# A hybrid trunk kernel: the recurrence's input and gate projections computed as a group of seven products among the projections of the attention branch

## The chip, the cores and the metric

One Trainium2 chip, one NeuronCore. The kernel is one launch of the whole two-layer trunk. The metric is device time in microseconds (us); the time before is the median of three runs, 1835.72 us (1835.08 to 1836.69). Engines are named as in the profile: PE is the matmul engine, PEld its weight loads, DVE the vector engine, ACT the scalar (activation) engine, POOL the general-purpose engine, which here mostly issues DMAs, and SP the engine that only issues DMAs. Each engine executes its own instructions in program order and waits, at an instruction, for semaphores of the others.

## The reference, cut to what matters

Two layers over 256 tokens of width 2048, in fp32. In each layer one wide projection of the normed rows is split into the inputs of four branches, and every branch result is gated, projected, and summed:

```python
def hybrid_layer(x, ...):
    h = rms_norm(x, norm_g)
    u = h @ w_in                                   # 256 x 2048 times 2048 x 15944
    (a_q, a_k, a_v, a_z, a_qi, a_ki, a_wi, b_q, b_k, b_v, b_z,
     c_f, c_i, c_q, c_z, m_q, m_z, gates) = split_cols(u)
    y_a = sparse_index_attention(...a_q, a_k, a_v, a_qi, a_ki, a_wi)
    y_b = head_rms_norm(retention(rope(b_q), rope(b_k), b_v), ret_g)
    f = lb + (1.0 - lb) * sigmoid(c_f)
    y_c = head_rms_norm(hgrn2(f, c_i, c_q), hgrn_g)          # the recurrence
    y_m = memory_attention(m_q, m_k, m_v)
    for n, (y, z) in enumerate(((y_a, a_z), (y_b, b_z), (y_c, c_z), (y_m, m_z))):
        branch = y * silu(z)
        merged += sigmoid(gates[n]) * (branch @ w_branch[n])
    return x + merged @ w_out
```

The change is about `c_i` (the recurrence's input) and `c_z` (its gate), each 256 x 2048 times 2048 x 512.

## The kernel before

**Slabs and halves.** Weights are streamed from HBM in slabs of 512 rows by 512 columns (1 MB, tile `raw`, four buffers, loaded on SP). Each slab is cut into two halves. For a half, ACT rounds the weights to `whi` (`ac.copy` in `cut_piece`) and DVE subtracts to get the remainder `wlo`; a plain projection then takes, for each of four 128-row blocks of its k and token half, three matmuls of 128x512: hi by hi, hi by lo, lo by hi. That is 12 matmuls a half, output tile `u`. `whi` and `wlo` have four buffers (HL), so the cut of a half can start only when PE has finished the half four places before it. The rows x are kept as `x00h`, `x00l`, and so on (layer, quarter of the 2048, rounded part and remainder).

**Groups of seven products.** For three of the four branches, two of the four column blocks of the gates are computed as one 2 x 2 block product with seven products instead of eight (output tile `px`). The weight combinations, tiles `sum`, are built in place by DMAs: the first block by a plain load on SP, further blocks by accumulating DMAs on POOL, each of which waits for DVE's cut of the tile that it changes (`add_block`). The combinations of x are called s1, s2, r4 and s3 and are made once a layer by `forms`: tile `s`, then a rounded part on ACT (`s1h`, `s2h`, `r4h`, `s3h`) and a remainder on DVE (`s1l`, ...). The s3 form is made in a second, later task. A product is used in two parts of two halves; a half takes 6 matmuls.

**Order.** Python records the program while it runs an account of engine costs. `gemms` and `product` record the matmuls of a half and then call `advance`, which lets the waiting tasks record up to two steps, and then records the cut of the next half. All side work (norms, transposes by DMA called `fold`, selection `ix...`, the recurrence's scores `cq`, `ck`, `cV`, `cin`, retention scores `bs`) is such tasks. `stream.finish(task)` records all that is left of a task at once. What has been recorded is the order on each engine; nothing is rearranged later. The program order of a layer is: the pair CF and CQ, then CI, CZ, QI0 (256 columns wide), QI1 (328), AQ, AK, AV, AZ, MQ, MZ, BQ, BK, BV, BZ, then the gates with their products and the branch projections `bw`, then the output projection `wo`.

**The retention scores.** `bs` is the product of `bqpt` and `bkpt`, two tiles that a `fold` moves in 16 small DMAs each, half on POOL and half on SP. SP's queue also holds the `raw` loads, which wait for the cut that frees their buffer.

Of the kernel before, what the change touches and what calls it, by code (L numbers as in the profile page):

```python
# [235 lines left out]

def mingled(products, side):
    out, total = [], sum(BETWEEN_PRODUCTS) * len(products) // 14
    at = done = 0
    for i in range(len(products) // 2):  # L240
        at += BETWEEN_PRODUCTS[i % 7]
        between = side[done:at * len(side) // total]
        done += len(between)
        inside = between[:len(between) // 2]
        out += [products[2 * i]] + inside + [products[2 * i + 1]] + between[len(inside):]
    return out


def gate_tokens():
    rows, products = [], []  # L250
    for n in BR_ORDER:
        gates = [[("gate", n, d, b) for b in range(4)] for d in range(4)]
        bridges = [("bridge", n, d) for d in range(4)]
        if n in DUO:
            products += [("product", n, i, part) for i in range(7) for part in range(2)]
# [10 lines left out]
def gemm_plan(wmem, win, wbr, wout):  # L266
# [15 lines left out]
    def product(l, n, i, part):  # L282
        stage = CHAINED[i]
        if stage is None:
            slab(win, gate_at(l, n, 2) + (2 + part) * 512 * 512, 512)
            return
        if stage == part == 0:
            starts[len(cuts) - AHEAD] = l, n
        cuts.extend(((l, n), stage, 2 * part + k) for k in range(2))
# [28 lines left out]
def trunk(ctx: ExitStack, tc: tile.TileContext, x, xt, memt, ng, qkg, hg, lbl, win, wmem, wbr, wout,  # L318
# [72 lines left out]
    def split_weights():  # L391
        if stream.cut in starts:
            group = starts[stream.cut]
            chains[group] = [G([128, 2, 512], "sum") for h in range(4)]
            for h in range(4):
                add_block(group, 0, h)
        if cuts[stream.cut]:
            group, stage, h = cuts[stream.cut]
            cut_piece(*half(512), chains[group][h])
            if stage + 1 < len(STAGES):  # L400
                add_block(group, stage + 1, h)
            return
# [4 lines left out]
        cut_piece(hi, lo, raw[:, 2 * j:2 * j + 2, :])  # L407
# [3 lines left out]
    def add_block(group, stage, h):  # L411
        adds, rows, d = STAGES[stage]
        to = chains[group][h].rearrange("p k n -> p (k n)")
        block = dram(win, gate_at(*group, d) + (2 * rows + h // 2) * 512 * 512 + h % 2 * 1024, 2048, 1024)
# [626 lines left out]
    def first_turned(b):  # L1041
# [4 lines left out]
        return split_scaled(raw, ngs[:, 0, 4 * b:4 * b + 4], xtp, "xt", f"x0{b}")  # L1046
# [84 lines left out]
    for l in range(L):  # L1131
# [24 lines left out]
        def loaded_tables(l=l):  # L1156
            yield from stream.rest(60)
            made = [spool.tile([128, 1024], F32, tag="s", name=f"table{i}") for i in range(2)]
# [4 lines left out]
        tables = stream.add(loaded_tables())  # L1163
        br = {}
        early = []
        gates_at = stream.ticks + sum(n for c, n in CHUNKS[:16]) / 64

# [13 lines left out]
        box[key("ci")] = evac(proj(O_CI), rs, "ci")  # L1181
        box[key("cz")] = gate_path(proj(O_CZ), rs, "cz")

        def forms(last=False, key=key):
            made = []

            def held(b, t):
                return [u[:, :, 128 * t:128 * t + 128].bitcast(F32) for u in xh[b]]

            def total(name, first, *signed):  # L1190
                out = first or G([128, 8, 128], name)
                for p in range(2):
                    to = out[:, 4 * p:4 * p + 4, :]
                    terms = [(u, sign) for sign, b, t in signed for u in held(b + p, t)]
                    if first is None:
                        (h, _), (g, sign), *_ = terms[::2]
                        (ve.tensor_add if sign > 0 else ve.tensor_sub)(to, h, g)
                        terms = terms[1::2]
                    for u, sign in terms:
                        yield  # L1200
                        (ve.tensor_add if sign > 0 else ve.tensor_sub)(to, to, u)
# [6 lines left out]
                return out  # L1208

            if last:  # L1210
                yield from wait_for(box, key("bs"))
                yield from total("s3", None, (1, 0, 0), (-1, 0, 1))
                return made
            s1 = yield from total("s1", None, (1, 0, 1), (-1, 2, 1))
            s2 = yield from total("s2", s1, (-1, 0, 0))
            yield from total("r4", s2, (1, 2, 0))
# [6 lines left out]
        stream.add(keep(key("aq"), normed_t(proj(O_AQ), rs, qks[:, l, 0:1], "aq")))  # L1223
        stream.add(keep(key("ak"), normed_t(proj(O_AK), rs, qks[:, l, 1:2], "ak")))
        br[0] = stream.add(attend(box, [key(n) for n in ("aq", "ak", "av", "az", "ix")], "a", gates_at + 40))
        box[key("av")] = evac(proj(O_AV), rs, "av")
        stream.add(keep(key("az"), transposed(gate_path(proj(O_AZ), rs, "az"), "azt")))
# [11 lines left out]
        ready += [stream.add(forms(True))]  # L1239
# [13 lines left out]

        def sigmoid(gt, t, src, rs=rs):
            ac.activation(gt[:, t, :], src, AF.Sigmoid, scale=rs[:, t:t + 1])
# [23 lines left out]
        def plain(b, t):  # L1279
            def form(k):  # L1280
                return [u[:, k % 4, 128 * t:128 * t + 128] for u in xh[b + k // 4]]
            return form

        def summed(i):
            def form(k):
                return [u[:, k, :] for u in ready[i // 3][i % 3]]
            return form

        groups, gates, open_gates = {}, {}, {}

        def open_group():
            stream.claim()
            return PB("px").rearrange("p (t n) -> p t n", t=2), {}, []

        def combined(qs, us, one, ended):
            ve.tensor_tensor(qs, qs, us[:, 0:1, :].to_broadcast([128, 2, 512]), op=OP.subtract)
            yield
            ve.tensor_tensor(us, qs, us[:, 1:2, :].to_broadcast([128, 2, 512]), op=OP.add)
            for t in range(2):
                yield  # L1300
                sigmoid(us, t, us[:, t, :])
            while not ended:
                yield BLOCKED
            ve.tensor_sub(one[:, 1, :], one[:, 1, :], qs[:, 1, :])
            yield
            sigmoid(one, 1, one[:, 1, :])
            return one, us

        FORMS = (lambda: summed(2), lambda: summed(3), lambda: plain(0, 0), lambda: summed(0), lambda: plain(2, 0),
                 lambda: summed(1), lambda: plain(2, 1))  # L1310

        def take(n, i, part):
            if i == part == 0:
                groups[n] = open_group()
            ps, kept_q, ended = groups[n]
            to = ps[:, (0, 1, 0, 1, 0, 1, 0)[i], :]
            product(to, FORMS[i](), part, i != 4, i == 4)
            if not part:
                return
            name = {0: "qs", 2: "us", 4: "gate"}.get(i)  # L1320
            if name:
                kept_q[name] = G([128, 2, 512], name)
            if i in (0, 2, 3, 6):
                name, t = {0: ("qs", 0), 2: ("us", 0), 3: ("us", 1), 6: ("gate", 1)}[i]
                ac.copy(kept_q[name][:, t, :], to)
            elif i == 1:
                ac.activation(kept_q["qs"][:, 1, :], to, AF.Copy, scale=-1.0)
            elif i == 4:
                sigmoid(kept_q["gate"], 0, to)
            else:  # L1330
                us = kept_q["us"]
                ve.tensor_add(us[:, 0, :], to, us[:, 0, :])
                task = stream.add(combined(kept_q["qs"], us, kept_q["gate"], ended))
                gates[n, 2], gates[n, 3] = (task, 0), (task, 1)
            if i == 6:
                ended.append(True)
                del groups[n]
                stream.free()

# [6 lines left out]
        for what, n, *at in gate_tokens():  # L1346
            if what == "product":
                for j, task in enumerate(ready):
                    if isinstance(task, Task) and (j == 0 or at[0]):
                        ready[j] = stream.finish(task)  # L1350
# [6 lines left out]
        def turned(c, xc, nssq, l=l):  # L1357
            u = yield from transposed(xc, "xp")
            r = split_scaled(u, ngs[:, l + 1, 4 * c:4 * c + 4], xtp, "xt", f"x1{c}")
            for t in range(2):  # L1360
# [81 lines left out]
```

## Time and profile before

| | |
|---|---|
| median of 3 runs | 1835.72 us (1835.08 to 1836.69) |
| the profiled execution's own time | 1837.45 us |
| its span, first to last instruction | 1835.7 us |
| mean granted PE clock | 0.999 |
| PE busy | 1825.5 us, 99% |
| DVE busy | 1286.2 us, 70% |
| ACT busy | 972.8 us, 53% |
| POOL busy | 337.1 us, 18% |
| moved by DMA | 428.38 MB, mean 233 GB/s |

The profiled execution took 1.73 us more than the median of the runs. PE is busy all through, so the time is nearly the sum of its matmuls, and the other engines matter only where PE waits for them. A busy duration of a matmul contains its pipeline, so the step from one matmul's start to the next is shorter than its duration; for the chain of work, pieces of many matmuls give the step.

### The profile page before, as it was taken

Reading aid. Unit: us, or ns where it says so; the run is one execution under the profiler, and the core shown is the slowest. Engines: PE = TensorE matmul, PEld = TensorE weight load, DVE = VectorE, ACT = ScalarE, POOL = GpSimd, SP = SyncE. Lnnn points to the kernel's source line nnn. Section 1 sums busy time; section 2 is a strip of 40 time slices with the busy share of each in tenths; the row PEclk is TensorE's granted clock in tenths of the full one; section 3 lists DMA queues with packets and bytes.
Section 4 is the critical chain, followed back from the end, with each engine's and each line's share of the span. In section 5 each row is a group of like instructions: output and inputs, shape, how many; then the busy total and the mean of one; then the engine's idle time right before and its main releaser. Section 6 shows DMA issues by size and latency. Waiting matters only on the chain.

```text
span 1835.7 us, 24214 instructions
## 1 busy us (share of the span) xinstructions
PE 1825.5 (99%) x8932; PEld 1518.1 (83%) x8932; DVE 1286.2 (70%) x1406; ACT 972.8 (53%) x1139; POOL 337.1 (18%) x501
## 2 busy tenths in 40 slices
PE   9999999999999999999999999999999999999999
PEld 8888888888888888888888888888888888888887
DVE  5655878777666767687665587887766676768764
ACT  5654555545365656554445454554545565555542
POOL 0022024214021011103131201421402111110310
PEclk9999999999999999999999999999999999999999
DMA  8776668778699898987797566886869989898873
GB/s 333 271 235 171 235 212 212 217 209 210 199 252 274 251 254 264 262 232 222 234 267 236 167 232 210 212 237 210 216 203 275 259 250 260 257 259 239 219 238 140
DMA packets 186568, 428.38 MB, mean 233 GB/s; under 512 B 114256, under 2 KB 115536, under 8 KB 150608
## 3 DMA queue, kind: packets, MB, share of 16 engines
q1 hardware_dynamic: 160048, 364.27, 61.3%
q0 software_dynamic: 26112, 62.29, 18.3%
q8 instruction: 70, 1.15, 0.3%
q14 instruction: 50, 0.41, 0.1%
q10 hardware_dynamic: 288, 0.26, 0.0%
HBM read 397.64 MB, written 5.24 MB: 219 GB/s over the span
## 4 chain that ended last, share of the span: by engine, by line
PE 93%; DMA 3%; DVE 1%; ACT 1%; issue 1%; SPq 0%; POOL 0%; DVEq 0%; ACTq 0%
PE u L145 57%; PE px L145 11%; PE bw L145 10%; PE wo L145 8%; PE mv L145 2%; PE mk L145 2%; DMA raw<-in_win 1%; DMA xp<-xpi 1%; DVE wlo L127 1%; ACT whi L127 1%; DMA bkpt<-bkpti 0%; DMA apT<-apT1i 0%; PE bs L145 0%; PE ixrp L145 0%; PE mlg L145 0%
## 5 line engine op out<-in xcount | busy, mean ns | idle before, releaser
L127 DVE TENSOR_TENSOR wlo<-raw,whi 128x1024 fp32r<-128x1024 f32 (+3 forms) x604 | 714.7, 1189 | 421.2 <-ACT whi L127 413.1
L127 ACT CAST whi<-raw 128x1024 fp32r<-128x1024 f32 (+3 forms) x604 | 620.1, 1029 | 684.7 <-PE u L145 460.8
L127 DVE TENSOR_TENSOR wlo<-sum,whi 128x1024 fp32r<-128x1024 f32 x144 | 174.0, 1223 | 63.6 <-ACT whi L127 58.6
L127 ACT CAST whi<-sum 128x1024 fp32r<-128x1024 f32 x144 | 151.3, 1055 | 86.4 <-PE u L145 39.4
L127 POOL DMA_DIRECT2D sum<-in_win x96 | 83.5, 870 | 520.1 <-DVE wlo L127 514.4
L145 PE MATMUL u<-whi,x03h 128*128 128x512 f32 (+2 forms) x208 | 80.0, 385 | 0.0
L145 PE MATMUL u<-whi,x13h 128*128 128x512 f32 (+2 forms) x208 | 80.0, 385 | 0.0
L145 PE MATMUL u<-wlo,x00h 128*128 128x512 f32 (+2 forms) x208 | 79.6, 383 | 0.2 <-DVE wlo L127 0.2
L145 PE MATMUL u<-whi,x10h 128*128 128x512 f32 (+2 forms) x208 | 79.8, 384 | 0.0
L145 PE MATMUL u<-wlo,x10h 128*128 128x512 f32 (+2 forms) x208 | 79.6, 383 | 0.2 <-DVE wlo L127 0.2
L145 PE MATMUL u<-whi,x00h 128*128 128x512 f32 (+2 forms) x208 | 79.8, 384 | 0.0
L145 PE MATMUL u<-whi,x02h 128*128 128x512 f32 (+2 forms) x208 | 79.8, 384 | 0.0
L145 PE MATMUL u<-whi,x12h 128*128 128x512 f32 (+2 forms) x208 | 79.8, 384 | 0.0
L145 PE MATMUL u<-whi,x01h 128*128 128x512 f32 (+2 forms) x208 | 79.7, 383 | 0.0
L145 PE MATMUL u<-whi,x11h 128*128 128x512 f32 (+2 forms) x208 | 79.7, 383 | 0.0
L145 PE MATMUL u<-wlo,x13h 128*128 128x512 f32 (+2 forms) x208 | 79.5, 382 | 0.0
L145 PE MATMUL u<-whi,x13l 128*128 128x512 f32 (+2 forms) x208 | 79.5, 382 | 0.0
L145 PE MATMUL u<-wlo,x01h 128*128 128x512 f32 (+2 forms) x208 | 79.5, 382 | 0.0
L145 PE MATMUL u<-wlo,x11h 128*128 128x512 f32 (+2 forms) x208 | 79.5, 382 | 0.0
L145 PE MATMUL u<-whi,x00l 128*128 128x512 f32 (+2 forms) x208 | 79.5, 382 | 0.0
L145 PE MATMUL u<-wlo,x12h 128*128 128x512 f32 (+2 forms) x208 | 79.5, 382 | 0.0
L145 PE MATMUL u<-wlo,x02h 128*128 128x512 f32 (+2 forms) x208 | 79.5, 382 | 0.0
(507 smaller groups left out, 4265.8 us busy)
## 6 DMA issues: line engine op xcount, KB each, us to landing
raw<-in_win SPq DMA_DIRECT2D x204, 1024.0 KB, 5.6
sum<-in_win POOLq DMA_DIRECT2D x96, 512.0 KB, 7.7
raw<-in_wbr SPq DMA_DIRECT2D x32, 1024.0 KB, 6.6
raw<-in_wout SPq DMA_DIRECT2D x32, 1024.0 KB, 5.9
sum<-in_win SPq DMA_DIRECT2D x48, 512.0 KB, 7.0
raw<-in_wmem SPq DMA_DIRECT2D x12, 1024.0 KB, 5.1
raw<-in_win SPq DMA_DIRECT2D x8, 656.0 KB, 4.4
xc<-in_x SPq DMA_DIRECT2D x8, 512.0 KB, 6.8
```

What stands on the lines that cost most here:

```text
L127: return call(*args, **kw)
L145: return self.engine.matmul(out, w, x, **kw)
```

## The change

For each layer, CI and CZ are no longer plain projections. They become a group "c" of seven products, with the same forms of x that the gate groups use. The group's products are put among QI0, QI1, AQ, AK, AV and AZ after the first four slabs (all of QI0, `EARLY`). CI and CZ are left out of the order between CQ and QI0.

- `forms` is one task, with s3 included. It reads x in fp32: the tile of x (`xr`, in the second layer `xp`) is scaled in place on ACT by a task `scaling` and kept, so a form takes one DVE operation per half tile, where it took one for the rounded parts and one more for each remainder. `take` finishes the task before the layer's first product.
- The product that runs on a plain slab moves from place 4 to place 5 of a group (`RING`). In group "c" the last block of the weight sum is added by DVE from that slab, and not by a DMA.
- The two tables of the retention scores sit in general buffers and are loaded at a set tick.
- `retain` rests one more tick; the numbers of side rows between products (`BETWEEN_PRODUCTS`) differ.

In all PE has 48 matmuls of 128x512 fewer (384 of `u` go, 336 of `px` come). DVE has 24 cuts of slabs fewer and 48 cuts of sums more, 24 form operations fewer and 8 additions to sums more; ACT has 24 and 48 such cuts, and 32 scalings of 128x256 more. POOL has 24 accumulating DMAs more, SP 12 slab loads fewer and 16 loads of a sum's first block more.

```diff
-STAGES = ((False, 1, 3), (True, 0, 3), (False, 0, 2), (True, 0, 3), (True, 1, 3), (True, 1, 2))
-CHAINED = (0, 1, 2, 3, None, 4, 5)
-BETWEEN_PRODUCTS = (4, 3, 4, 3, 2, 4, 3)
+STAGES = ((False, 1, 1), (True, 0, 1), (False, 0, 0), (True, 0, 1), (True, 1, 1))
+LAST_SUM, RING, EARLY = (True, 1, 0), 5, 4
+BETWEEN_PRODUCTS = (4, 3, 4, 4, 3, 2, 3)
...
+def columns(l, group):
+    if group == "c":
+        return [l * DM * INW + CHUNK_AT[c] for c in (O_CI, O_CZ)]
+    return [gate_at(l, group, d) for d in (2, 3)]
...
+def early_tokens():
+    rows = [("chunk", c, n, b) for c, n in CHUNKS[4:10] for b in range(4)]
+    return rows[:EARLY] + mingled(products_of("c"), rows[EARLY:])
...
         pair(PAIR_ORDER, *((win, l * DM * INW + CHUNK_AT[c]) for c in (O_CF, O_CQ)))
-        for c, n in CHUNKS[2:16]:
+        for what, *at in early_tokens():
+            if what == "product":
+                product(l, *at)
+            else:
+                c, n, b = at
+                slab(win, l * DM * INW + CHUNK_AT[c] + b * 512 * n, n)
+        for c, n in CHUNKS[10:16]:
             add(win, l * DM * INW + CHUNK_AT[c], n)
...
+        piece = raw[:, 2 * j:2 * j + 2, :]
+        cut_piece(hi, lo, piece)
+        if group and group[1] == "c":
+            ve.tensor_add(chains[group][h], chains[group][h], piece)
...
-        return split_scaled(raw, ngs[:, 0, 4 * b:4 * b + 4], xtp, "xt", f"x0{b}")
+        r = split_scaled(raw, ngs[:, 0, 4 * b:4 * b + 4], xtp, "xt", f"x0{b}")
+        stream.add(scaling(raw, 0, b))
+        return r
+
+    def scaling(u, l, b):
+        for k in range(4):
+            if k % 2 == 0:
+                yield
+            ac.activation(u[:, k, :], u[:, k, :], AF.Copy, scale=ngs[:, l, 4 * b + k:4 * b + k + 1])
+        rows_of[l, b] = u
...
         def retain():
             q = yield from wait_for(box, key("bq"))
             k = yield from wait_for(box, key("bk"))
+            yield from stream.rest(1)
...
-        box[key("ci")] = evac(proj(O_CI), rs, "ci")
-        box[key("cz")] = gate_path(proj(O_CZ), rs, "cz")
...
+            def total(name, out, sign, first, second):
+                for p in range(2):
...
+                    yield
+                    (ve.tensor_add if sign > 0 else ve.tensor_sub)(at, a, b)
+
+            def parts(name, out):
+                hi, lo = (spool.tile([128, 8, 128], F32R, tag="s", name=name + e) for e in "hl")
+                yield
+                ac.copy(hi, out)
+                yield
+                ve.tensor_sub(lo, out, hi.bitcast(F32))
+                made.append((hi, lo))
...
+            one = G([128, 8, 128], "s1")
+            yield from total("s1", one, -1, a21, a22)
+            yield from parts("s1", one)
+            yield from total("s2", one, -1, one, a11)
+            yield from parts("s2", one)
+            yield from total("r4", one, 1, one, a12)
+            yield from parts("r4", one)
+            yield from total("s3", one, -1, a11, a21)
+            yield from parts("s3", one)
...
         ready = [stream.add(forms())]
...
+        def take(group, i, part):
+            if isinstance(ready[0], Task):
+                ready[:] = stream.finish(ready[0])
...
+            form = (summed(2), summed(3), plain(0, 0), summed(0), summed(1), plain(2, 0), plain(2, 1))[i]
+            product(to, form, part, i != RING, i == RING)
...
+        def early_slabs(c0, n=512, l=l):
+            tiles = None
+            for b in range(4):
+                while tokens[0][0] == "product":
+                    take(*tokens.popleft()[1:])
...
+                tiles = gemms(xh, [(win, l * DM * INW + CHUNK_AT[c0])], n, ["u"], order=[(0, b, j) for j in range(2)], tiles=tiles)
+            return tiles[0]
...
-        qi0 = evac(proj(O_QI, 256), rs, "qi0", 256)
-        qi1 = evac(proj(O_QI + 256, 328), rs, "qi1", 328)
+        qi0 = evac(early_slabs(O_QI, 256), rs, "qi0", 256)
+        qi1 = evac(early_slabs(O_QI + 256, 328), rs, "qi1", 328)
...
-        ready += [stream.add(forms(True))]
```

The next rows are the order of instructions, first on DVE from the end of QI0's cuts (128x512) into QI1's (128x656) in the first layer, as the program was; `s_1526` is the tile in which the forms are built, `cq`, `cown` and `ck` belong to the recurrence.

```order
61 L127 TENSOR_TENSOR wlo<-raw,whi 128x512 x4
62 L127 SCALAR_TENSOR_TENSOR czzs<-u,rs0r,czsg 128x512 x2
63 L127 TENSOR_TENSOR s_1526<-x00h,x02h 128x512
64 L127 TENSOR_TENSOR wlo<-raw,whi 128x512 x2
65 L127 TENSOR_TENSOR s_1526<-s_1526,x00l 128x512
66 L127 TENSOR_TENSOR wlo<-raw,whi 128x512 x2
67 L127 TENSOR_TENSOR s_1526<-s_1526,x02l 128x512
68 L127 TENSOR_TENSOR wlo<-raw,whi 128x656
69 L127 TENSOR_TENSOR s_1526<-x01h,x03h 128x512
70 L127 TENSOR_TENSOR wlo<-raw,whi 128x656
71 L127 TENSOR_TENSOR cq<-cq_1432,cf 128x1024
72 L127 TENSOR_TENSOR s_1526<-s_1526,x01l 128x512
```

A form's operations stood singly between the cuts. The same place of the changed program; here `s_1219` is the tile of the forms, and the last row's cuts are of the third and fourth block of the group's first sum.

```order
60 L127 TENSOR_TENSOR wlo<-raw,whi 128x512
61 L127 TENSOR_TENSOR wlo<-sum,whi 128x1024 x2
62 L127 TENSOR_TENSOR s1l<-s_1219,s1h 128x1024
63 L127 TENSOR_TENSOR wlo<-raw,whi 128x656 x2
64 L127 TENSOR_TENSOR s_1219<-s_1219,xr 128x512 x2
65 L127 TENSOR_TENSOR s2l<-s_1219,s2h 128x1024
66 L127 TENSOR_TENSOR s_1219<-s_1219,xr 128x512 x2
67 L127 TENSOR_TENSOR r4l<-s_1219,r4h 128x1024
68 L127 TENSOR_TENSOR s_1219<-xr 128x512 x2
69 L127 TENSOR_TENSOR s3l<-s_1219,s3h 128x1024
70 L127 TENSOR_TENSOR wlo<-sum,whi 128x1024 x2
```

All of s2, r4 and s3 now stands in one piece behind two cuts of QI1's first slab. On PE of the changed program the first product follows the last matmul of QI0, and its first matmuls read `r4h` and, in the third, `r4l`:

```order
677 L145 MATMUL u<-whi,x03h 128x256
678 L145 MATMUL u<-wlo,x03h 128x256
679 L145 MATMUL u<-whi,x03l 128x256
680 L145 MATMUL px<-whi,r4h 128x512
681 L145 MATMUL px<-wlo,r4h 128x512
682 L145 MATMUL px<-whi,r4l 128x512
```

Where QI0 was followed by QI1, the first product now stands between them. SP's queue in the first layer, before BZ ends, with the moves of `bkpt` (for the retention scores) and the slab loads, as it was:

```order
114 L521 DMA mpT_3905<-mpT1i 32x8x32
115 L521 DMA bkpt<-bkpti 32x8x32 x2
116 L374 DMA raw<-in_win 128x2048
117 L521 DMA bkpt<-bkpti 32x8x32 x5
118 L374 DMA raw<-in_win 128x2048
119 L521 DMA bkpt<-bkpti 32x8x32
```

and as it is:

```order
112 L545 DMA apT_3847<-apT1i 32x8x32 x5
113 L393 DMA raw<-in_wbr 128x2048
114 L545 DMA bkpt<-bkpti 32x8x32 x5
115 L393 DMA raw<-in_win 128x2048
116 L545 DMA bkpt<-bkpti 32x8x32 x3
```

The last slab load ahead of the last move of `bkpt` waits for a cut. Before, the half of that cut is used by PE 11 matmuls of 128x512 ahead of `bs`; now 47 such matmuls ahead (with 8 small ones of the attention), and in the second layer 59 where it was 11. Last, DVE in the first layer just before the fifth product's result is taken up (`us<-px`), where the additions to the sums stand:

```order
136 L127 TENSOR_TENSOR wlo<-raw,whi 128x1024 x2
137 L127 TENSOR_TENSOR cq<-cq,cT_2136 128x256x2
138 L127 TENSOR_TENSOR ck<-ck,cT_2136 128x256x2
139 L127 TENSOR_TENSOR cT_2317<-cT_2136 128x256
140 L127 TENSOR_TENSOR wlo<-raw,whi 128x1024
141 L127 TENSOR_TENSOR sum<-sum,raw 128x1024
142 L127 TENSOR_TENSOR wlo<-raw,whi 128x1024
143 L127 TENSOR_TENSOR sum<-sum,raw 128x1024
144 L127 TENSOR_TENSOR us<-px,us 128x512
```

The rows `sum<-sum,raw` and this place of `us<-px` are new; the recurrence's operations of the kernel before stood among cuts of plain slabs and the forms.

More of the change, by code (lines that the diff above doesn't have):

```diff
@@ L254, in gate_tokens @@
         if n in DUO:
-            products += [("product", n, i, part) for i in range(7) for part in range(2)]
+            products += products_of(n)
         if n == BR_ORDER[-1]:
@@ L280, in pair, with product @@
             slab(src, off + b * 512 * 512, 512)
[L282 to L289, printed above, removed]
+    def product(l, group, i, part):
+        if i == RING:
+            p.append((win, columns(l, group)[0] + (2 + part) * 512 * 512, 512))
+        elif i == part == 0:
+            starts[len(cuts) - AHEAD] = l, group
+        cuts.extend(((l, group), i, 2 * part + k) for k in range(2))
     for b in range(4):
@@ L1153, in retain, with loaded_tables @@
             k = yield from wait_for(box, key("bk"))
+            yield from stream.rest(1)
             return (yield from retention_scores(q, k, "b", tables.value))
-        def loaded_tables(l=l):
-            yield from stream.rest(60)
-            made = [spool.tile([128, 1024], F32, tag="s", name=f"table{i}") for i in range(2)]
+        def loaded_tables(until):
+            while stream.ticks < until:
+                yield BLOCKED
+            made = [G([128, 1024], f"table{i}") for i in range(2)]
             for i, to in enumerate(made):
@@ L1180, in trunk, with forms @@
         br[2] = stream.add(mixed("cs", "ci", "cz", 1, "c", gates_at + 3))
-        box[key("ci")] = evac(proj(O_CI), rs, "ci")
-        box[key("cz")] = gate_path(proj(O_CZ), rs, "cz")
-        def forms(last=False, key=key):
+        def forms(l=l):
+            rows = []
+            for b in range(4):
+                rows.append((yield from wait_for(rows_of, (l, b))))
             made = []
[L1187 to L1191, printed above, removed]
+            def total(name, out, sign, first, second):
                 for p in range(2):
[L1193 to L1201, printed above, removed]
+                    at, a, b = (u[p] if isinstance(u, tuple) else u[:, 4 * p:4 * p + 4, :] for u in (out, first, second))
                     yield
+                    (ve.tensor_add if sign > 0 else ve.tensor_sub)(at, a, b)
+            def parts(name, out):
                 hi, lo = (spool.tile([128, 8, 128], F32R, tag="s", name=name + e) for e in "hl")
+                yield
                 ac.copy(hi, out)
@@ L1207, in total @@
                 made.append((hi, lo))
[L1208 to L1216, printed above, removed]
+            a11, a12, a21, a22 = (tuple(rows[b + p][:, :, 128 * t:128 * t + 128] for p in range(2))
+                                  for t in range(2) for b in (0, 2))
@@ L1221, in trunk, with sigmoid, scale_rows, plain @@
[L1221 removed]
+        def sigmoid(gt, t, src):
+            ac.activation(gt[:, t, :], src, AF.Sigmoid, scale=rs[:, t:t + 1])
+        def scale_rows(u, t, src):
+            ac.activation(u[:, t, :], src, AF.Copy, scale=rs[:, t:t + 1])
+        def plain(b, t):
+            def form(k):
+                return [u[:, k % 4, 128 * t:128 * t + 128] for u in xh[b + k // 4]]
+            return form
+        def summed(i):
+            def form(k):
+                return [u[:, k, :] for u in ready[i]]
+            return form
@@ new lines, in trunk, with open_group, combined @@
+        groups, gates, open_gates = {}, {}, {}
+        def open_group():
+            stream.claim()
+            return PB("px").rearrange("p (t n) -> p t n", t=2), {}, []
+        def combined(parts, ended, first, second):
+            qs, us = parts["qs"], parts["us"]
+            ve.tensor_tensor(qs, qs, us[:, 0:1, :].to_broadcast([128, 2, 512]), op=OP.subtract)
+            yield
+            ve.tensor_tensor(us, qs, us[:, 1:2, :].to_broadcast([128, 2, 512]), op=OP.add)
+            yield
+            second = yield from second(us)
+            while not ended:
+                yield BLOCKED
+            one = parts["one"]
+            ve.tensor_sub(one[:, 1, :], one[:, 1, :], qs[:, 1, :])
+            yield
+            first(one, 1, one[:, 1, :])
+            return one, second
@@ new lines, in both, with gated_path @@
+        def both(us):
+            for t in range(2):
+                sigmoid(us, t, us[:, t, :])
+                yield
+            return us
+        def gated_path(us):
+            yield
+            return gate_path(us, rs, "cz")
+        def take(group, i, part):
+            if isinstance(ready[0], Task):
+                ready[:] = stream.finish(ready[0])
+            if i == part == 0:
+                groups[group] = open_group()
+            ps, parts, ended = groups[group]
+            first, second = (scale_rows, gated_path) if group == "c" else (sigmoid, both)
+            to = ps[:, (0, 1, 0, 1, 1, 0, 1)[i], :]
+            form = (summed(2), summed(3), plain(0, 0), summed(0), summed(1), plain(2, 0), plain(2, 1))[i]
+            product(to, form, part, i != RING, i == RING)
+            if not part:
+                return
+            name = {0: "qs", 2: "us", RING: "one"}.get(i)
+            if name:
+                parts[name] = G([128, 2, 512], name)
+            if i in (0, 2, 3, 6):
+                name, t = {0: ("qs", 0), 2: ("us", 0), 3: ("us", 1), 6: ("one", 1)}[i]
+                ac.copy(parts[name][:, t, :], to)
+            elif i == 1:
+                ac.activation(parts["qs"][:, 1, :], to, AF.Copy, scale=-1.0)
+            elif i == RING:
+                first(parts["one"], 0, to)
+            else:
+                us = parts["us"]
+                ve.tensor_add(us[:, 0, :], to, us[:, 0, :])
+                task = stream.add(combined(parts, ended, first, second))
+                gates[group, 2], gates[group, 3] = (task, 0), (task, 1)
+            if i == 6:
+                ended.append(True)
+                del groups[group]
+                stream.free()
@@ new lines, in trunk, with from_group @@
+        tokens = deque(early_tokens())
+        def early_slabs(c0, n=512, l=l):
+            tiles = None
+            for b in range(4):
+                while tokens[0][0] == "product":
+                    take(*tokens.popleft()[1:])
+                assert tokens.popleft() == ("chunk", c0, n, b)
+                tiles = gemms(xh, [(win, l * DM * INW + CHUNK_AT[c0])], n, ["u"], order=[(0, b, j) for j in range(2)], tiles=tiles)
+            return tiles[0]
+        def from_group():
+            task, _ = gates[("c", 2)]
+            while not task.done:
+                yield BLOCKED
+            box[key("ci")], box[key("cz")] = task.value
@@ L1295, in combined @@
[L1295 to L1338, printed above, removed]
```

51 lines of the change are left out of this document (21 added, 30 removed).

## The prediction

> **What bounds the kernel now.** I read the page's busy times first, then PE's waits, then the chain that ended last, and only then single stretches of the timeline.
>
> ```profile
> PE 1825.5 (99%) x8932; PEld 1518.1 (83%) x8932; DVE 1286.2 (70%) x1406; ACT 972.8 (53%) x1139; POOL 337.1 (18%) x501
> PE bs L145 <- DMA apT<-apT1i: 3.4, 2, 2.5
> PE heat L145 <- DVE warm L127: 1.1, 1, 1.1
> PE wo L145 <- DVE wlo L127: 0.5, 1, 0.5
> ```
>
> The second to fourth lines are waits: total, times, longest. PE is busy 99% of the span, and the only wait of PE worth naming is that of `bs`. So two things can move the time: the number of matmuls, and any stall that PE does not have now. In the chain that ended last, a product of one part and a plain slab read:
>
> ```profile
> 510.12 2.75 PE px L145 x12
> 512.87 5.44 PE u L145 x24
> ```
>
> (start, us, what). 24 matmuls of 128x512 in 5.44 us are 226.7 ns each, and 12 of a product take 2.75, so a product's matmul costs what a plain one does.
>
> **Fewer matmuls.** 384 of `u` go and 336 of `px` come: 48 x 0.2267 = 10.9 us less on PE, which is the path. This term is the surest of all.
>
> **The wait of `bs`.** In the timeline of PE (and SP's queue) around it, first layer and then second:
>
> ```profile
> 457.06 0.93 SPq L521 DMA_DIRECT2D bkpt<-bkpti  x1
> 462.81 0.39 PE L145 MATMUL u<-whi,x03l 128*128 128x512 f32 x1
> 465.65 3.46 PE L145 MATMUL bs<-bqpt,bkpt 128*128 128x256 f32 x8 [2.45 <-DMA apT<-apT1i]
> 468.77 0.58 PE L145 MATMUL bw<-whi,cnh 128*128 128x512 f32 x1
> 1334.26 0.39 PE L145 MATMUL u<-whi,x13l 128*128 128x512 f32 x1
> 1335.56 1.97 PE L145 MATMUL bs<-bqpt,bkpt 128*128 128x256 f32 x8 [0.91 <-DMA apT<-apT1i]
> 1337.17 0.59 PE L145 MATMUL bw<-whi,cnh 128*128 128x512 f32 x1
> ```
>
> A matmul that starts at 462.81 makes way 0.23 later, at 463.04, so PE stood idle 2.61 us; in the second layer, from 1334.49, 1.07. There is a second price. The same eight records took 3.12 us until `bw` began in the first layer and 1.61 in the second: 1.51 more, half speed after an idle of 2.61 and none after 1.07. Together 5.2 us. The releaser that the row names is in the same queues as `bkpt`, which `bs` reads; its last move was issued at 457.06. In the new order the slab load ahead of that move waits for a cut that lies 36 matmuls farther ahead of `bs` in the first layer (47 against 11) and 48 in the second: 8.2 and 10.9 us more lead against 2.61 and 1.07 of wait. I take the wait as gone, -5.2. Ends: -5.2, and 0 if some other move is late there instead.
>
> **The forms, in front of the first product.** This is the term that decides. In the new order on DVE, s2, r4 and s3 stand in one piece behind the two cuts of 128x656. The second of those cuts needs the buffer of QI0's last half, so ACT can start it only when PE has finished that half; call this moment T. But PE's next matmul after T is the first product, which reads `r4h`, and its third reads `r4l`. PE must wait from T until s2, its two parts, r4 and its two parts are made one after another. In the kernel before, the forms' operations stood singly between cuts and were needed only some 320 us later by the gates. The rows:
>
> ```profile
> L127 ACT CAST whi<-raw 128x656 fp32r<-128x656 f32 x16 | 11.9, 744 | 10.9 <-PE u L145 10.7
> L127 ACT CAST r4h<-s 128x1024 fp32r<-128x1024 f32 x2 | 2.1, 1042 | 0.0
> L127 DVE TENSOR_TENSOR wlo<-raw,whi 128x656 fp32r<-128x656 f32 x16 | 13.0, 834 | 1.0 <-ACT whi L127 1.0
> L127 DVE TENSOR_TENSOR s<-s,x01l 128x512 f32<-128x512 f32 x4 | 2.7, 684 | 0.0
> L127 DVE TENSOR_TENSOR s1l<-s,s1h 128x1024 fp32r<-128x1024 f32 x2 | 2.4, 1218 | 0.0
> L127 DVE TENSOR_TENSOR r4l<-s,r4h 128x1024 fp32r<-128x1024 f32 x2 | 2.4, 1218 | 0.0
> ...
> 179.78 0.28 PE L145 MATMUL u<-whi,x00l 128*128 128x256 f32 x1
> 180.50 0.28 PE L145 MATMUL u<-whi,x00l 128*128 128x256 f32 x1
> ...
> 189.16 0.84 DVE L127 TENSOR_TENSOR wlo<-raw,whi 128x656 fp32r<-128x656 f32 x1
> 189.92 1.22 DVE L127 TENSOR_TENSOR cq<-cq,cf 128x1024 f32<-128x1024 f32 x1
> ...
> 209.01 1.22 DVE L127 TENSOR_TENSOR wlo<-raw,whi 128x1024 fp32r<-128x1024 f32 x1
> 210.14 0.68 DVE L127 TENSOR_TENSOR s<-s,x00l 128x512 f32<-128x512 f32 x1
> 210.74 1.22 DVE L127 TENSOR_TENSOR wlo<-raw,whi 128x1024 fp32r<-128x1024 f32 x1
> ```
>
> The first six are groups (busy, mean ns of one). The others are starts: operations of DVE that do not depend on each other follow at 1.13 (from 209.01 to 210.14) for 1.22, 0.60 for 0.68, 0.76 for 0.84; a dependent one waits the full duration. A half of QI0 is 12 matmuls of 0.12 (six steps from 179.78 to 180.50), 1.4 us, about the 1.22 of a cut of a sum: so DVE comes to T with the two cuts of sums just done and `s1l` running, by my count with 0.85 of it left. From there: 0.85 + 2 x 0.76 for the cuts, s2 0.60 + 0.68, `s2h` 1.04 on ACT, `s2l` 1.22, r4 0.60 + 0.68, `r4h` 1.04, `r4l` 1.22: 9.45, and five changes of engine or dependent starts of some 0.03 make 9.6. Without the forms the third matmul would have come 0.45 after T, so PE loses 9.1 in each layer, 18.2 in both. Lower end, with `s1l` and the first of the cuts done at T: 0.74 + 0.83 + 7.08 - 0.45 = 8.2. Upper end, with all of `s1l` behind T and no overlap: 9.85. s3 follows on DVE, but behind the first part PE has two ready halves of QI1, and s3's 3.5 us and the next cut fit in; nothing is added.
>
> **The clock behind that stall.** `bs` lost 1.51 after 2.61 us of idle, so after 9 us I add 1.5 for each layer, 3.0. Ends: 0, and 1.7 each, since the program's start ran at half speed for about 3.4 us:
>
> ```profile
> 1.12 3.35 PE L145 MATMUL heat<-warm 128*128 128x128 f32 x14 [1.12 <-DVE warm L127]
> ```
>
> The Trainium skill, page "TensorE: Matmul & The Clock Gate", Part 1, has a clock that falls to half after at least one idle window of about 3.4 us and is granted in full after one busy window of the same length. The `bs` row differs for the fall, since 2.61 us of idle had sufficed. By the page's rule the removal of `bs`'s wait would be worth 3.7 and not 5.2, and the sum below would come out 1.5 higher; I go by the row.
>
> **DVE between the fourth and the fifth product.** DVE gets more here: cuts of sums, additions to sums, and at the same time selection and recurrence. The longest run without slack that I find in the new order goes from behind a cut of a sum to `us<-px`, for which PE's sixth product waits: 14 cuts, 2 additions, 16 steps of selection, 21 others.
>
> ```profile
> L127 DVE TENSOR_TENSOR wlo<-raw,whi 128x1024 fp32r<-128x1024 f32 x565 | 686.7, 1220 | 404.4 <-ACT whi L127 396.4 <-DMA apT<-apT0i 3.0 <-DMA mgp<-mgpi 1.5
> L127 DVE TENSOR_TENSOR acc<-acc,gate 128x1024 f32<-128x1024 f32 x18 | 22.0, 1225 | 0.6
> L127 DVE SCALAR_TENSOR_TENSOR ixsc<-ixrl,ixw,ixsc 128x128 f32<-128x128 f32 x14 | 4.9, 352 | 0.5
> L127 DVE MAX8 ixm<-ixsc 128x8 f32<-128x128 f32 x16 | 4.6, 285 | 0.0
> ...
> L145 PE MATMUL ixrp<-ixkt,ixqt 64*32 64x128 f32 x128 | 2.3, 274 | 0.0
> L145 PE MATMUL cl<-cV,ck 128*32 128x48 f32 x256 | 3.5, 208 | 0.0
> L145 PE MATMUL cdg<-cown,ones 128*32 128x256 f32 x16 | 1.3, 391 | 0.0
> ...
> 184.00:194.00 10.00, 10.00 (x81) 10.00 (x80) 9.79 (x14) 5.71 (x9) 0.00 (x0) 1.00 0.81 263
> ```
>
> 16 x 1.22 = 19.6; selection 8 x 0.35 + 8 x 0.28 = 5.1; the others, 3 of a full tile at 1.22, 7 of half a tile at 0.68 and 11 of an estimated 0.35, 12.3: 37 us, behind 2.3 for the first cut's release. PE has 156 matmuls (35.4) and half of `ixrp`'s 2.3, a quarter of `cl`'s 3.5 and about 1.1 of `cdg`: 38.5. So DVE would be 0.8 late by durations, and on time by starts, which come some 0.08 earlier for about half of them. The last row (a window; third number after the bar of times: DVE) shows DVE 9.79 of 10 us busy with PE at 10.00. I take 0; ends 0 and 2 for both layers.
>
> **What else moves.** ACT's 24 more cuts, 32 scalings and table loads lie beside PE: ACT is 53% busy and PE never waits for it. POOL's 24 more accumulating DMAs and SP's 16 loads wait in the queues in which the `fold` moves stand too:
>
> ```profile
> sum<-in_win POOLq DMA_DIRECT2D x96, 512.0 KB, 7.7
> POOL sum L127 <- DVE wlo L127: 514.4, 79, 22.3
> ```
>
> A sum's block lands 7.7 us after its issue, and POOL stands waiting at such an issue for DVE's cut; moves behind it go later. Sums that are added to now have at least 15 us of PE's work until their next cut, by my count of the order, so they land in time. A late move costs what `bs` shows, 2.6 and 1.5. I take 0; ends 0 (a gain is excluded, since no wait of this kind is left to remove) and 8, two late moves.
>
> **The sum.** -10.9 - 5.2 + 18.2 + 3.0 = +5.1. The sum stands on the profiled execution, whose span is 1835.7 and whose own time is 1837.45, 1.73 above the median of the runs; the difference is added to the median: 1835.7 + 5.1 = 1840.8 us.
>
> **The rivals.**
> - *Faster: the forms are hidden.* If r4 is made while QI0 still runs, only -10.9 - 5.2 are left: 1819.6. For it: in the trace a form's steps are recorded early and singly. Against it: the rows of the new order, in which the steps stand behind a cut that waits for T. It decides once the stall is below 6.2 us a layer, of which r4's part alone (0.60 + 0.68 + 1.04 + 1.22) is 3.5; s2's three steps would have to lie ahead of T. 0.12.
> - *No change.* The stall at its lower end, 16.4, with the clock's loss absent or small: -16.1 + 16.4 + (0 to 3.0) = +0.3 to +3.3, 1836 to 1839. For it: the ends of the two terms; against it: 1.51 after an idle a quarter as long. 0.23.
> - *Slower by far: late transfers take over the place of `bs`.* In the early group the recurrence's and the selection's moves share POOL with adds that wait. Two or three waits as long as that of `bs`, 4.1 each with its clock: 1840.8 + 8 to 12 = 1849 to 1853. For it: POOL's 514 us of waiting at these issues; against it: none of the gates' 96 such adds made PE wait. 0.15.
>
> **How the numbers follow.** My forecast, slower with the stall of the forms as its mark, has 0.50; its own range is 1839.4 to 1846. A change below 0.2%, 3.7 us, is about what a measurement of this kernel cannot tell from none. Slower: 0.50 + 0.15 = 0.65; within 0.2%: 0.23; faster: 0.12. The range leaves out most of the hidden case below and the worst of late transfers above: 1831 to 1851.
>
> **What would show it.** In the changed profile: a wait of PE at `px` for `r4h` or `r4l` (ACT or DVE), two times, 8 to 10 us each, near 150 us and near 1010; half clock in PE's row behind each; no wait at `bs`; no wait at `px` for `us<-px` above 1 us; the chain in time with pieces of DVE `r4l` and `s2l`. I am wrong if PE runs through from `u` 128x256 to `px`, if `bs` still waits, or if waits for DMAs at the recurrence or the selection appear.

## The result, and the profile after

The changed kernel took 1858.58 us (median of four runs, 1857.49 to 1860.1) against 1836.2 us; ratio 1.012, 95% interval 1.0102 to 1.0137. It is slower by 22.4 us, 1.2%. The forecast was slower, 1840.8, range 1831 to 1851: the sign is right, the size missed by 17.8 us. The profiled executions differ by 20.5 us in their spans (1835.7 and 1856.2). Of the thirteen runs of the kernel before that were timed beside run 10 below, two were in a slower state (2018.53 and 3740.36 us) and are left out of its comparison.

The page's busy times and PE's waits of the changed kernel (total, times, longest):

```profile
PE 1822.1 (98%) x8884; PEld 1512.2 (81%) x8884; DVE 1316.0 (71%) x1422; ACT 1019.4 (55%) x1209; POOL 361.0 (19%) x525
PE px L145 <- ACT r4h L127: 16.7, 2, 8.6
PE u L145 <- DVE wlo L127: 6.2, 3, 5.5
PE wo L145 <- DVE gate L127: 1.7, 1, 1.7
PE px L145 <- DVE us L127: 1.6, 1, 1.6
PE alg L145 <- ACT akpt L127: 1.0, 1, 1.0
```

PE has 48 records fewer, and `bs` no longer appears among the waits. Two new ones are large: the wait for `r4h`, once a layer, and one of DVE's cuts. The first in the timeline of DVE, ACT and PE:

```profile
147.95 1.22 DVE L127 TENSOR_TENSOR s1l<-s,s1h 128x1024 fp32r<-128x1024 f32 x1
149.09 1.59 DVE L127 TENSOR_TENSOR wlo<-raw,whi 128x656 fp32r<-128x656 f32 x2
150.59 1.29 DVE L127 TENSOR_TENSOR s<-s,xr 128x512 f32<-128x512 f32 x2
152.99 1.23 DVE L127 TENSOR_TENSOR s2l<-s,s2h 128x1024 fp32r<-128x1024 f32 x1 [1.11 <-ACT s2h L127]
156.66 1.23 DVE L127 TENSOR_TENSOR r4l<-s,r4h 128x1024 fp32r<-128x1024 f32 x1 [1.11 <-ACT r4h L127]
148.55 0.74 ACT L127 CAST whi<-raw 128x656 fp32r<-128x656 f32 x1 [0.65 <-PE u L145]
155.58 1.04 ACT L127 CAST r4h<-s 128x1024 fp32r<-128x1024 f32 x1 [2.62 <-DVE s L127]
148.23 0.28 PE L145 MATMUL u<-whi,x03l 128*128 128x256 f32 x1
156.68 0.79 PE L145 MATMUL px<-whi,r4h 128*128 128x512 f32 x1 [8.17 <-ACT r4h L127]
157.94 0.79 PE L145 MATMUL px<-whi,r4l 128*128 128x512 f32 x1
160.66 0.63 PE L145 MATMUL px<-whi,r4l 128*128 128x512 f32 x1
161.09 0.63 PE L145 MATMUL px<-whi,r4h 128*128 128x512 f32 x1
```

QI0 makes way on PE at 148.35; `r4l` starts 8.31 later, and the third matmul 9.59 later, as the chain had been added up (9.97 later in the second layer). Matmuls then follow at 0.43 instead of 0.227 until 161.9: half speed for 5.3 us. The second wait lies in the second layer, in DVE's rows and then PE's:

```profile
1091.15 1.23 DVE L127 TENSOR_TENSOR wlo<-raw,whi 128x1024 fp32r<-128x1024 f32 x1 [1.96 <-ACT whi L127]
1099.69 1.23 DVE L127 TENSOR_TENSOR cq<-cq,cf 128x1024 f32<-128x1024 f32 x1 [7.32 <-DMA ixqt<-ixqti]
1100.84 1.21 DVE L127 TENSOR_REDUCE aqss<-aqsq 128x8 f32<-128x1024 f32 x1
1102.16 3.49 DVE L127 TENSOR_TENSOR wlo<-raw,whi 128x1024 fp32r<-128x1024 f32 x3
1097.58 0.39 PE L145 MATMUL u<-whi,x11h 128*128 128x512 f32 x1
1103.44 0.79 PE L145 MATMUL u<-wlo,x11h 128*128 128x512 f32 x1 [5.46 <-DVE wlo L127]
```

DVE stands 7.32 us at the recurrence's multiplication, whose input `cq` has been moved by DMA (the releaser named is a move of another tile that landed within 0.1 us of the last one of `cq`); the cuts queue behind it, and PE stops. In the first layer the same multiplication waits 5.00, without PE stopping. How long the 32 moves of that tile take from issue to landing, before and after, and one row of a table by stretch for each (in order: PE, PEld, DVE, ACT, POOL, then PE's clock, DMA share, GB/s):

```profile
DMA to landing us min/median/max: 1.9/3.1/4.5
DMA to landing us min/median/max: 5.3/7.9/15.4
...
1065.00:1100.00 35.00, 35.00 (x254) 30.46 (x253) 30.29 (x45) 18.77 (x24) 4.24 (x8) 1.00 0.68 237
1065.00:1100.00 35.00, 32.97 (x146) 26.95 (x144) 18.87 (x21) 19.43 (x20) 18.73 (x29) 1.00 1.02 233
```

The DMA engines are busy all the time there (1.02 against 0.68) and move no more than before (233 GB/s against 237). The kernel before moves its `cq` of that layer earlier, in the stretch from 1036 to 1052 us, where the share was 0.54. That load is what the prediction lacked.

**The ledger.** Matmuls -10.9, `bs` -5.2. The forms: 148.23 to 162.18 is 13.95 us for steps that take 2.84, so 11.1 lost; in the second layer, 1023.12 to 1036.80, 10.8. The late `cq`: 5.6 of idle and 2.0 at half speed, 7.6. `us` 1.7, `gate` at `wo` 1.9 (a wait of 0.7 at another place of `wo` is gone), `alg` 1.1. Sum +17.4 of the 20.5 of the spans; the other 3.1 us were not traced. The expectations of the experiments below were written with 11.4 and 11.1 for the forms and 8.3 for `cq`, somewhat more than this count.

### The profile page after: what moved, and what is told of

Its sections match the earlier page's. It is cut to its first block, busy times and chain, and to the rows that moved or that the text cites. A ratio compares the mean times of both kernels' runs of the same rounds, so it can differ in the third digit from the quotient of the medians.

```text
span 1856.2 us, 24285 instructions
## 1 busy us (share of the span) xinstructions
PE 1822.1 (98%) x8884; PEld 1512.2 (81%) x8884; DVE 1316.0 (71%) x1422; ACT 1019.4 (55%) x1209; POOL 361.0 (19%) x525
## 4 chain that ended last, share of the span: by engine, by line
PE 89%; DVE 5%; DMA 3%; ACT 1%; issue 1%; SPq 0%; ACTq 0%; DVEq 0%
PE u L145 49%; PE px L145 14%; PE wo L145 9%; PE bw L145 9%; DVE wlo L127 2%; PE mv L145 2%; PE mk L145 2%; DMA cq<-cq0i 1%; ACT whi L127 1%; DMA raw<-in_win 0%; DVE ixsc L127 0%; DMA ixqt<-ixqti 0%; SPq L545 0%; PE mlg L145 0%; PE mov L145 0%
## 5 line engine op out<-in xcount | busy, mean ns | idle before, releaser
L127 DVE TENSOR_TENSOR wlo<-raw,whi 128x1024 fp32r<-128x1024 f32 (+3 forms) x580 | 685.8, 1189 | 401.2 <-ACT whi L127 393.4
L127 ACT CAST whi<-raw 128x1024 fp32r<-128x1024 f32 (+3 forms) x580 | 593.2, 1026 | 631.2 <-PE u L145 406.5
L127 DVE TENSOR_TENSOR wlo<-sum,whi 128x1024 fp32r<-128x1024 f32 x192 | 232.1, 1223 | 66.6 <-ACT whi L127 59.3
L127 ACT CAST whi<-sum 128x1024 fp32r<-128x1024 f32 x192 | 201.2, 1053 | 115.0 <-PE u L145 62.1
L127 POOL DMA_DIRECT2D sum<-in_win x120 | 108.3, 903 | 637.8 <-DVE wlo L127 631.8
L145 PE MATMUL u<-whi,x11l 128*128 128x512 f32 (+2 forms) x192 | 74.0, 385 | 0.0
L145 PE MATMUL u<-whi,x03h 128*128 128x512 f32 (+2 forms) x192 | 73.6, 383 | 0.0
L145 PE MATMUL u<-whi,x00h 128*128 128x512 f32 (+2 forms) x192 | 73.5, 383 | 0.0
L145 PE MATMUL u<-whi,x10h 128*128 128x512 f32 (+2 forms) x192 | 73.4, 383 | 0.0
L145 PE MATMUL u<-whi,x02h 128*128 128x512 f32 (+2 forms) x192 | 73.4, 382 | 0.0
```

What stands on the lines that cost most here:

```text
L127: return call(*args, **kw)
L145: return self.engine.matmul(out, w, x, **kw)
```

## The experiments

Runs 7 and 10 were timed four and ten times, the others once. Four runs of the changed kernel differ by 2.6 us and the four of run 7 by 6.4, so smaller differences between single runs show nothing.

**1 to 4: the two waits, each alone and together.** First, the forms' task is started before CF and CQ:

```diff
+        ready = [stream.add(forms())]
         early.append(rs)
         gemms(xh, [... for c in (O_CF, O_CQ)], ...)
...
-        ready = [stream.add(forms())]
```

> The forms' task is started before CF and CQ, so that s2 and r4 stand between earlier cuts; all else is the changed kernel. Theory one (the two waits for r4 cost 11.4 and 11.1 us, idle and half clock together): both waits vanish, 1858.6 - 22.5 = about 1836. Rival (the forms' work is only moved and DVE holds PE elsewhere): less than half of that, over 1847.

It took 1860.48, no gain at all. In the second layer nothing moved (the steps came no earlier in its order: x itself is finished only at the layer's start), and the 8.6 us stayed. In the first layer the wait for `r4h` was gone, and another, in which PE stood idle for 6.1 us, came 18 us later (DVE, then PE; the last row is DVE in the changed kernel):

```profile
160.86 1.23 DVE L127 TENSOR_TENSOR wlo<-sum,whi 128x1024 fp32r<-128x1024 f32 x1 [1.25 <-ACT whi L127]
171.50 1.38 DVE L127 TENSOR_SCALAR cf<-cf,olb,lbv 128x256 f32<-128x256 f32 x4 [9.41 <-DMA raw<-in_win]
172.80 1.22 DVE L127 TENSOR_TENSOR wlo<-sum,whi 128x1024 fp32r<-128x1024 f32 x1
166.13 0.40 PE L145 MATMUL px<-whi,s3l 128*128 128x512 f32 x1
172.46 0.80 PE L145 MATMUL px<-whi,s3h 128*128 128x512 f32 x1 [5.92 <-ACT whi L127]
...
191.26 1.38 DVE L127 TENSOR_SCALAR cf<-cf,olb,lbv 128x256 f32<-128x256 f32 x4 [1.15 <-ACT cf L127]
```

The recurrence's other moved tile, `cf`, lands late too: up to 15.4 us after its issue, 11.8 in the changed kernel and 7.2 in the kernel before. But the edit also moved the operation that waits. DVE takes `cf` up behind 7 cuts after `s3l` in run 1 and behind 17 in the changed kernel, at 171.5 us and at 191.3: with the forms recorded early, the recurrence's steps are recorded earlier too (in the second layer, where the forms did not move, it stays at 17). So this wait came with the edit, and nothing here shows that the forms' stall had hidden it. What the forms' two waits are worth alone stays open; a run that takes them away and leaves `cf` in its place was not made.

Second, the recurrence takes up its moved q later:

```diff
         q0 = yield from transposed(uq, name + "q0")
+        yield from stream.rest(4)
```

> Changed kernel, but the recurrence takes up its moved q tile four ticks later, so that DVE does not stand waiting for the moves. Theory one (the stall of 8.3 us near 1098 us in the second layer is DVE held up at one operation by transfers that land late): it vanishes, about 1850, the forms' waits unchanged. Rival (DVE has too much work there): the stall stays within 2 us of its size, about 1858.

1851.36, 7.2 less, and the wait at the cut is gone (PE waits for DVE's cuts of `u` 0.4 in all); the forms' 16.7 is unchanged. DVE's amount of work is the same, so it was one operation that waited, with the cuts behind it. The moves still land late (up to 14.5 us); nothing waits for them any more.

Third, the cause of the late landing:

```diff
-        if adds:
+        if adds and group[1] == "c":
+            po.dma_start(to, block)
+        elif adds:
             po.dma_start(to, block, accum_op=OP.add)
```

> Changed kernel, but the early group's accumulating DMAs are plain loads of the same blocks from the same queue, at the same places and with the same waits; its sums are left out. If the moves land late because accumulating loads the DMA engines, the q moves land in under 6 us (9.1 in the changed kernel), DVE's wait for them falls under 2 us in both layers and the stall of 8.3 is gone, about 1850. If they are late because they stand behind waiting instructions in the queues, the landing stays above 8 us and the time at about 1858.

1848.36, 10.2 less. DVE no longer waits at `cq`, PE not at the cut. The software queue and the other one in the same stretch of the second layer, first of the changed kernel and then of this one (MB, share of 16 engines), and the moves' landing:

```profile
q0 software_dynamic: 1566, 3.67, 53.8%
q1 hardware_dynamic: 4708, 4.46, 47.5%
...
q0 software_dynamic: 1568, 3.67, 36.8%
q1 hardware_dynamic: 4788, 4.97, 50.8%
DMA to landing us min/median/max: 4.9/6.7/8.7
```

The same 3.67 MB (six blocks of the sums and the moves issued on POOL) take 53.8% of the DMA engines when the blocks accumulate and 36.8% when they are plain, 5.1 and 3.5 us for a MB, and with them go the longest landings, from 15.4 to 8.7. The median fell only from 7.9 to 6.7, not under 6 as the first theory had it. The place in the queue seems to have a part in it as well. In the second layer of the changed kernel the last move of `cq` on SP was issued 0.6 us behind a slab load, and two on POOL were issued within 1 us of it (KB each, us to landing):

```profile
raw<-in_win SPq DMA_DIRECT2D x1, 1024.0 KB, 10.4
cq<-cq0i SPq DMA_DIRECT2D x1, 32.0 KB, 14.9
cq<-cq0i POOLq DMA_DIRECT2D x2, 32.0 KB, 6.9
```

The move on SP was issued at 1084.70, so it landed at 1099.6, and DVE goes on at 1099.69. So it is this one move that DVE waited for. Run 3 shows that without the load of accumulating nothing is late enough to be waited for; that the slab ahead of the move has a part in it is argued from these rows. Whether issuing the move ahead of the slab would do as much as taking the load away was not run.

Fourth, the first two edits together:

> Both edits, forms early and q later. If the two stalls are separate, the gains add: 1858.6 - 22.5 - 8.3 = about 1828, faster than the kernel before by 8. If one makes room for the other, above 1834.

1851.89. The gains did not add: the first layer's wait behind `cf` (6.2), which came with the edit of run 1, and the second layer's for `r4h` (8.6) are the two that remain.

**5: DVE's additions.**

```diff
-        if group and group[1] == "c":
-            ve.tensor_add(chains[group][h], chains[group][h], piece)
...
-            elif i == 4 and group[1] != "c":
+            elif i == 4:
                 add_block(group, LAST_SUM, h)
```

> Changed kernel, but the last block of the early group's sums is added by an accumulating DMA, as in the gate groups, and not by DVE (8 DVE additions of 1.2 us fewer, 8 accumulating DMAs of 512 KB more). If DVE's work is what holds PE at the sixth product of the first layer (1.7 us), that wait falls under 0.5 and the time by 1 to 2, about 1857. If accumulating DMAs are what costs in this stretch, new late transfers add more than that: 1860 and over.

1857.18 in one run. The wait for `us` is gone from PE's list (1.6 before), so DVE's run up to `us` did hold PE; the wait for `gate` grew from 1.7 to 2.4. The 1.4 less in the time is within what single runs of one kernel differ by (2.6 for the changed kernel), so a gain is not shown.

**6: the extra tick.**

```diff
             k = yield from wait_for(box, key("bk"))
-            yield from stream.rest(1)
```

> Changed kernel without the extra tick in the retention scores' task. If the order of the moves alone gives the lead (47 and 59 matmuls against 11), no wait appears at bs and the time stays at about 1858. If the tick is what removed it, a wait of 1 to 3 us comes back at bs, with half clock 1859 to 1862.

1858.97, and no wait at `bs`. So the tick is not what removed that wait. What is left is the order of the moves, as the prediction's count of 47 and 59 matmuls against 11 had it; the new order of products with the old order of moves was not run.

**7 and 8: products later.** The forms early, `f` and `q` of the recurrence taken up four ticks later, and the first product after ten slabs instead of four, or after eight:

```diff
-LAST_SUM, RING, EARLY = (True, 1, 0), 5, 4
+LAST_SUM, RING, EARLY = (True, 1, 0), 5, 10
```

> Forms' task before CF and CQ, first product after ten slabs instead of four (all of QI0 and QI1 and two of AQ), and the recurrence takes up both its moved tiles, f and q, four ticks later. Theory one: the forms' two waits and the waits behind moved tiles vanish, what is left is the saved matmuls and the wait of bs, minus small waits at DVE of 2 to 6 us: 1836 - 16 + 2 to 6 = 1822 to 1826, faster than before. Rival (the load on DVE and on the DMA engines of this stretch is the real price and only shows elsewhere): waits of 10 us or more in all at other places, 1830 to 1840.

1846.23 (ratio to the kernel before 1.0048, interval 1.0032 to 1.0065). Both waits for `r4h` are gone and so are those behind `cf` and `cq`. But:

```profile
PE ixrp L145 <- DMA aqpt<-aqpti: 7.9, 1, 7.9
PE mov L145 <- DVE mpl L127: 3.2, 1, 3.2
PE u L145 <- ACT whi L127: 3.0, 1, 3.0
```

The selection's product now waits for its moved q, ACT stands 7.37 at the attention's moved q with the cuts behind it, and the memory attention waits too. The rival of this run won, with 1846 even above its 1830 to 1840: here the price went to the next tiles that are moved.

> As the run above but with the first product after eight slabs; in the second layer r4 still stands behind the first cut that waits. Theory one: one wait for r4 of 3 to 5 us is left in the second layer and none in the first, some 4 to 7 us above the version with ten slabs.

1850.23, with one wait for `r4h`, in the second layer, as expected; at 5.6 it is a little longer than the 3 to 5 foreseen. The 4.0 above the median of the run with ten slabs are less than the four runs of that version differ by, so the difference in time is not shown.

**9 and 10: two ways to serve the moves.** The version with ten slabs with plain loads in place of the early group's accumulating DMAs:

> The version with forms early and the first product after ten slabs, but the early group's accumulating DMAs are plain loads of the same blocks (its sums are left out). If the load of the accumulating DMAs is the price that moved to other places, the waits behind moved tiles (8 us at the selection's product, 3.3 behind the q of the attention, 3.3 at the memory's) vanish or fall under 1 us each: 1846 - 15 to 20 = 1826 to 1831. If it is the order of the queues or DVE's work, above 1840.

1837.86, 8.4 less. The wait at the selection's product fell from 7.9 to 0.7, and ACT's at the attention's q from 7.4 to 1.6, so that PE no longer waits behind it; the memory attention's stayed (3.7), which lies among the gates, where the DMAs were left as they are. The expected 1826 to 1831 was missed, and the rival's 1840 was not reached. So the accumulating of the early group's DMAs costs PE the waits at its own moved tiles and not that of the memory attention. The share of the DMA engines in the two stretches from 195 and from 1065 us stayed full, 1.01 and 1.00 with plain loads against 1.07 and 1.02 with the sums: a full share alone does not tell whether a tile will be waited for.

The version with ten slabs with all sums, but four more moved tiles taken up later:

```diff
         while left:
             yield BLOCKED
-        yield from stream.rest(3)
+        yield from stream.rest(6 if name.startswith(('ixqt', 'mpT', 'aqpt', 'akpt')) else 3)
         return whole
```

> The same version with its sums, but the moved tiles of the selection's q, of the attention's q and k and of the memory's weights are also taken up three ticks later than now. If PE, ACT and DVE only wait because they take up tiles too soon, these waits vanish: 1826 to 1832, faster than the kernel before. If the DMA engines are full, part of the waits reappears at slab or sum loads, 1834 to 1842.

1834.07 against 1837.37 for the kernel before beside it, ratio 0.998, interval 0.9969 to 0.999: faster, by 3.3 us, and the only version here that is. That is less than the 3.7 us that the prediction took for the least that can be told from no change; only the number of runs sets it apart. PE's longest waits of it:

```profile
PE u L145 <- DVE wlo L127: 3.7, 5, 2.4
PE wo L145 <- DVE gate L127: 1.6, 1, 1.6
PE px L145 <- DVE us L127: 1.3, 1, 1.3
```

No wait for a moved tile above 0.4 us is left, although the DMA share in the stretch is above 1 (1.10 in the second layer). The time lies at the lower end of the second expectation, but not for its reason. The waits of 8 and 3 us did vanish, and PE's waits in the three rows, 6 to 7 us, are for DVE. Ahead of the longest of them (2.4, at 1122 us) DVE had stood 5.6 for a small operation on POOL, and not for a load, and was busy from there on. So of the saved 16.1 us of matmuls and `bs` some 3 are left when the transfers are given their time.

## Why the prediction was right or wrong

- **Fewer matmuls, -10.9:** right (8884 records against 8932).
- **The wait of `bs`, -5.2:** right, and not by the added tick (run 6); that it was the order of the moves is argued from the count.
- **The forms, 9.1 a layer:** right in place, mechanism and size; third matmul at T + 9.59 and, in the second layer, T + 9.97, against T + 9.6 in the count, so 9.1 and 9.5 lost ahead of it.
- **The clock, 1.5 a layer:** what was lost behind the third matmul came to 2.0 and 1.3 against 1.5 foreseen, and with the forms to 11.1 and 10.8 against 10.6.
- **DVE to `us`, 0:** the upper end was right: 1.7, in one layer of two.
- **"What else moves", 0:** this step failed. The late `cq` cost 7.6 us (5.6 idle, 2.0 at half speed), which is half of the 15.4 us by which the spans missed the sum. The step asked whether the sums that are added to land before their next cut; they do (ACT waits for them 1.8 us in all). It did not ask what their load does to the small moves that share the DMA engines. The rates were on the page of before (below): 5.4 us of the span for a MB of the software queue, 3.1 for one of the other. With the MB that the two traces have in the stretch of 35 us that was at 0.68, the first goes from 0.07 to 3.67 MB, which is 0.56 more, and the other from 8.21 to 4.46, which is 0.33 less: an estimated 0.9, where 1.02 was measured. I had priced two late waits at 8 us and kept them as a rival with 0.15; one late wait of nearly that size is what came. The sign that the prediction named for being wrong, waits for DMAs at the recurrence, appeared: DVE's 7.32 and 5.00 at `cq`. The argument against that rival, that the gates' adds made PE wait for nothing, was no ground for the early group; why the gates bear their adds was not tested. The two rows of the page of before (packets, MB, share of 16 engines' span):

```profile
q1 hardware_dynamic: 160048, 364.27, 61.3%
q0 software_dynamic: 26112, 62.29, 18.3%
```

- **The remainder:** 1.1 in `alg` and 1.2 more at `wo` are small waits at places that the prediction did not look at; the cause of the last 3.1 us of the spans stays open.

The sign did not depend on the failed step: without its 7.6 us the sum of the ledger is still 9.8 above zero. Half of the miss in size did depend on it.

## What to carry to other kernels

An edit that takes away the stall that is seen can bring another of nearly its size elsewhere, as in runs 1 and 7; before you say that the first had hidden the second, compare in both programs how many cuts stand ahead of the operation that waits. When a change adds accumulating DMAs, add up the DMA engines' time in that stretch, by queue and per MB from the page, and then look at the smallest transfers there, not at the large ones that were added, and at what is issued just ahead of them in their queue. Work whose result is first needed just after a point where the order blocks has to be recorded well ahead of that point.

## What the runs showed of the hardware that was not expected

- The software queue took 5.1 us of 16 engines' time for a MB with six accumulating blocks among its 3.67 MB, and 3.5 with plain loads of the same blocks (run 3).
- The granted clock after a short idle is not a matter of its length alone. An idle of 2.61 us (`bs` before) was followed by half speed; 1.89 at `wo` and 1.74 before the sixth product, in the changed kernel, were not. In the last version an idle of 2.55 was followed first by 1.3 us at full speed and then by 3.4 at half; in run 5 an idle of 2.54 at `wo` was followed by none. Between the program's start and PE's last matmul, every stretch of half speed in these traces lasts 3.4, 6.8 or 10.2 us. In the first layer of the changed kernel it set in at 151.7, 3.4 us after PE had stopped, and went on to 162.0. The Trainium skill, page "TensorE: Matmul & The Clock Gate", Part 1, says that the window of the gate runs freely. A half speed that sets in 1.3 us after work has begun again agrees with that. The idle window of about 3.4 us that the Trainium skill gives for the fall, read as a threshold on one idle, does not agree with 2.61.
